# Two FFNs with seven products over all row blocks, and the residual kept in DRAM

## Chip, cores and metric

One core of a Trainium2 chip. The metric is device time in microseconds, here a median of 3 runs. TensorE multiplies, ScalarE (ACT), VectorE (DVE) and GpSimd (POOL) work on elements, SyncE (SP) issues most DMAs. Each engine works through its own queue in order.

## The reference

Two transformer blocks over 1024 tokens of width 1024, in float32. What this change touches are the output projection of the first block's attention, and the two feed-forward networks (FFNs):

```
x = x + g1 * (concat(norm(o_a), norm(o_b)) @ w_out)            # output projection
x = x + g2 * ((silu(h @ w_gate) * (h @ w_up)) @ w_down)        # first FFN; h = modulated norm of x
x = x + gla(norm(x))                                           # second block's mixer
u = causal_conv3(norm(x) @ ffn_w_up) + b; g, val = split(u)    # second FFN
x = x + (silu(g) * val) @ ffn_w_down                           # then the final norm
```

Both FFNs have 2816 hidden columns: 11 groups of 256. Each full-precision product is three matmuls (high part by high, high by low, low by high), with every operand cut into a rounded high part and a rest.

## The kernel before, in words

**Residual and activations.** `X` holds the residual x as eight tiles of 128 rows in SBUF. `H[0]` and `H[1]` hold the high and low parts of the normed activations, transposed, as 8 blocks of 128 rows (k) by 1024 tokens.

**Weights (class `Weights`, L62).** `W` is a planner with a list of tasks in a fixed order: for each item a load of 1 MB into `raw` (one buffer, L159), then its pieces, then an end. A piece takes the next of the 8 slots of a ring (`ring`), if its owner has released it, and is cut there into high (ACT, L139) and low parts (DVE or POOL, L140). `W.tick(n)` emits up to n tasks at the place where it is called; a load is emitted with the tick that ends the item before it, and with `W.pause` the tick after a load does nothing. `need(idx, j)` and `get` emit at once what is still missing. Since `raw` is one buffer, a load waits on SP until the last piece of the item before has been cut. The order in an FFN is gate of g, down of g-1, up of g.

**FFN (`ffn`, L1451).** `first` computes group 0 of gate and up in plain products: tokens 0 to 511 first, then 512 to 1023. Groups 1 to 9 run as `seven(g, "g")`, `down(g - 1)`, `seven(g, "u")`. `seven` replaces the eight block products of [2 column halves x 2 row halves of the weights] by [2 row halves x 2 token halves of H] with seven products of sums (Winograd's form of Strassen's method). Before, that is done on k blocks 0 to 3 only (each product over 2 blocks); blocks 4 to 7 go as plain products: 14 + 16 = 30 block products of three matmuls, 90 in all. The weight sums are made by POOL (`_seven`, L100: 256 columns per operation), in 6 pieces. The sums over H are made once per FFN by `t_step0` to `t_step4` during `first`'s second half and the first `seven`, and overwrite part of H's second half; `restore` brings that back at group 9. The results are put together by DVE sums from PSUM (L1674), POOL sums (L1677) and ACT copies (L1670) in six buffers `uv`.

**Places in `seven`.** After each product stands `point(i)`: `STEPS` (L33) says how many waiting output stages it emits (`flush`: convolution taps, SiLU, multiplication, cutting of the hidden values) and how many weight tasks (`W.tick`):

```
(False, 'g'): ((2, 0), (0, 1), (0, 2), (0, 2), (1, 2), (1, 0), (1, 0)),
(False, 'u'): ((1, 1), (0, 1), (1, 0), (0, 1), (2, 2), (0, 2), (3, 1)),
(True, 'g'): ((4, 0), (3, 0), (0, 2), (2, 1), (3, 0), (0, 1), (0, 1)),
(True, 'u'): ((2, 2), (2, 1), (2, 1), (1, 1), (2, 3), (1, 1), (2, 0)),
```

False is the first FFN, True the second (with convolution).

**Down (L1668 on).** 16 outputs of 128x512, each 6 matmuls, added to `X` by `tm_add` (L1377): in the first FFN DVE multiplies by the gate and POOL adds; in the second DVE adds. `down_last` does groups 9 and 10 together and feeds the next norm.

**Output projection (L1427).** Four column quarters `n4`, each over 8 row tiles; the norm of the result (`Norm`, 14 steps) runs along the last quarter and into `first`.

Of the kernel before, what the change touches and what calls it, by code (L numbers as in the profile page):

```python
# [63 lines left out]
class Weights:  # L64
# [24 lines left out]
    def add7(self, load):  # L89


        idx = len(self.items)
        self.items.append({"load": load, "done": False, "slots": []})
        self.tasks.append(("load", idx, 0))
        for j in range(6):
# [117 lines left out]
def kernel(ctx: ExitStack, tc: tile.TileContext, a: dict, out: bass.AP, dbg=None):  # L213
# [1005 lines left out]
    xp = pool("x", "right", stack=st_x)  # L1219
    X = [xp.tile([P, D], F32, tag=f"x{t}", name=f"x{t}") for t in range(8)]  # L1220
    hp = pool("hT", "right", stack=st_x)
    H = [hp.tile([P, KD, S], R32, tag=f"h{i}", name=f"h_{i}") for i in range(2)]
    st_ps = ExitStack()
# [17 lines left out]
    class Norm:  # L1241
# [177 lines left out]
    nrm = Norm(dmod[2], lambda t, xh: to_fm(None, xh, t), dmod[1])  # L1419
# [7 lines left out]
    for n4 in range(4):  # L1427
# [8 lines left out]
        for t in range(8):  # L1436
# [21 lines left out]
    def ffn(tag, conv, grow, nrm, nxt):  # L1458
# [8 lines left out]
        W.tmp = fp.tile([P, 2, 2, P], F32, name="s12")  # L1467
# [107 lines left out]

# [3 lines left out]
        def hb(x, k, half):  # L1579
            return H[x][:, 2 * k:2 * k + 2, half * 512:half * 512 + 512]  # L1580

        def hf(x, k, half):
            return hb(x, k, half).bitcast(F32)

        def open_t():
            tp = pool("t" + tag, "right", stack=st_t)
            T["t"] = [tp.tile([P, 2, 2, 512], R32, name=f"t{x}") for x in range(2)]
            tp = pool("t2" + tag, "right", stack=st_t2)
            T["t2"] = [tp.tile([P, 2, 512], R32, name=f"t2{x}") for x in range(2)]
# [8 lines left out]
        def t_step0():  # L1598
            tt(nc.gpsimd, f3, hf(1, 0, 1), hf(1, 0, 0))
            tt(nc.vector, f1, hf(0, 0, 1), hf(0, 0, 0))  # L1600
            tt(nc.vector, f1, f1, f3, ALU.add)

        def t_step1():
            tt(nc.vector, f2, hf(0, 1, 1), f1)
            tt(nc.vector, f2, f2, hf(1, 1, 1), ALU.add)
            t_split(f2, *T["t2"])

        def t_step2():
            W.tick(2)
            tt(nc.vector, f3, f2, hf(0, 0, 0))  # L1610
            tt(nc.gpsimd, f3, f3, hf(1, 0, 0))
            tt(nc.vector, f2, hf(0, 1, 0), f2)
            tt(nc.gpsimd, f2, f2, hf(1, 1, 0), ALU.add)

        def t_step3():
            t_split(f1, *[hb(x, 0, 1) for x in range(2)])

        def t_step4():
            t_split(f3, *[t[:, 0] for t in T["t"]])
            t_split(f2, *[t[:, 1] for t in T["t"]])  # L1620
# [580 lines left out]
```

## Time and profile before

| what | value |
|---|---|
| median of 3 runs | 2676.56 us (2676.5 to 2678.79) |
| profiled execution, its own time | 2675.95 us |
| its span, first to last instruction | 2674.2 us |
| granted TensorE clock, mean | 0.991 |
| output projection | to 734 us |
| first FFN | 734 to 1467 us |
| second FFN | 1906 us to the end |

The span is what the trace covers; 1.75 us of the execution lie outside. In rows, L12 is line 12 of the kernel; `out<-in` are tile names; a number in square brackets is the idle time of the engine before that instruction, with what ended it. A group is one pass of the loop over g: one `seven` for up, one for the next gate, one `down`, as they follow each other from one end of a `down` to the next.

### The profile page before, as it was taken

The numbers are of one execution on the slowest core, as the hardware profiler recorded it, in microseconds if no ns is written. First come the engines' busy times: TensorE is split into PE (matmuls) and PEld (weight loads), VectorE is DVE, ScalarE is ACT, GpSimd is POOL, SyncE is SP. The second block draws the span as 40 slices with busy tenths as digits, with TensorE's granted clock in tenths as the row PEclk, the third lists the DMA queues.
The fourth block names the chain that finished last, engine by engine and source line by source line (L and its number), as shares of the span: only waits on it lengthen the run. The fifth ranks groups of instructions, "written<-read, shape, count | busy, mean of one in ns | idle before, by whom it ended". The sixth has DMA issues, their size and how long they took to land. (4 is left out here: it accounts for less than half of the span.)

```text
span 2674.2 us, 37149 instructions
## 1 busy us (share of the span) xinstructions
PE 2575.6 (96%) x14053; PEld 2152.5 (80%) x14053; DVE 1631.4 (61%) x3011; ACT 1057.8 (40%) x2613; POOL 1139.3 (43%) x1079
## 2 busy tenths in 40 slices
PE   8999999999899999999999999999999999999998
PEld 4999898899887888888878877877777777777786
DVE  4688678774475555555556442332777777777766
ACT  4644488784232222222223525232433333333333
POOL 2355255664446666666643111212333333333321
PEclk9999999999999999999999999999999999999999
DMA  6166422212101111111111111111101111111112
GB/s 244 33 194 203 144 52 68 64 44 88 56 17 48 63 48 48 54 57 48 48 48 56 35 48 32 48 32 48 40 32 48 48 48 48 48 48 48 48 48 87
DMA packets 152540, 170.87 MB, mean 64 GB/s; under 512 B 39444, under 2 KB 135460, under 8 KB 151336
## 3 DMA queue, kind: packets, MB, share of 16 engines
q1 hardware_dynamic: 152200, 168.35, 19.9%
q8 instruction: 111, 1.82, 0.3%
q0 software_dynamic: 160, 0.14, 0.1%
q14 instruction: 69, 0.57, 0.1%
HBM read 154.81 MB, written 13.65 MB: 63 GB/s over the span
## 5 line engine op out<-in xcount | busy, mean ns | idle before, releaser
L140 POOL TENSOR_TENSOR wlo<-raw,whi 128x512 fp32r<-128x512 f32 x132 | 178.8, 1359 | 449.1 <-ACT whi L139 420.2
L1656 PE MATMUL pgu<-h,whi 128*128 128x512 f32 x864 | 342.6, 397 | 3.1 <-DVE h L1592 3.1
L1657 PE MATMUL pgu<-h,wlo 128*128 128x512 f32 x864 | 341.2, 395 | 0.5 <-POOL wlo L140 0.5
L1655 PE MATMUL pgu<-h,whi 128*128 128x512 f32 x864 | 341.3, 395 | 0.0
L140 DVE TENSOR_TENSOR wlo<-raw,whi 128x512 fp32r<-128x512 f32 (+2 forms) x304 | 230.1, 769 | 153.4 <-ACT whi L139 152.8
L139 ACT ACTIVATE whi<-raw 128x512 fp32r<-128x512 f32 (+1 forms) x436 | 232.5, 552 | 170.9 <-DMA raw<-in_w_down 60.3
L1674 DVE TENSOR_TENSOR uv<-pgu,uv 128x512 f32<-128x512 f32 x216 | 148.3, 687 | 150.2 <-PE pgu L1657 129.2
L237 PE MATMUL pdn<-wlo,hid 128*128 128x512 f32 x576 | 227.3, 395 | 12.2 <-DVE wlo L140 12.2
L236 PE MATMUL pdn<-whi,hid 128*128 128x512 f32 x576 | 226.3, 393 | 1.2 <-DVE uv L1383 1.1
L238 PE MATMUL pdn<-whi,hid 128*128 128x512 f32 x576 | 226.5, 393 | 0.0
L1384 POOL TENSOR_TENSOR x<-x,uv 128x512 f32<-128x512 f32 x144 | 192.2, 1356 | 32.2 <-DVE uv L1383 29.3
L1656 PEld LDWEIGHTS pgu<-h,whi 128*128 128x128 f32 x864 | 162.2, 188 | 42.3 <-DVE h L1592 3.6
L1655 PEld LDWEIGHTS pgu<-h,whi 128*128 128x128 f32 x864 | 162.5, 188 | 40.1
L1657 PEld LDWEIGHTS pgu<-h,wlo 128*128 128x128 f32 x864 | 162.2, 188 | 39.9 <-POOL wlo L140 0.9
L1525 POOL TENSOR_TENSOR hid<-sg,hid 128x512 fp32r<-128x512 f32 x80 | 106.8, 1340 | 194.3 <-ACT hid L1524 192.2
L1677 POOL TENSOR_TENSOR uv<-uv 128x512 f32<-128x512 f32 x72 | 106.4, 1478 | 162.9 <-DVE uv L1674 162.9
L236 PE MATMUL pin<-whi,h 128*128 128x256 f32 x512 | 145.5, 284 | 5.4 <-ACT hsq L634 2.2
L237 PE MATMUL pin<-wlo,h 128*128 128x256 f32 x512 | 145.6, 284 | 1.7 <-DVE wlo L140 1.7
L238 PE MATMUL pin<-whi,h 128*128 128x256 f32 x512 | 145.7, 285 | 0.0
L1524 ACT ACTIVATE hid<-sg 128x512 fp32r<-128x512 f32 x80 | 50.3, 632 | 231.9 <-DVE sg L1522 231.9
L237 PEld LDWEIGHTS pdn<-wlo,hid 128*128 128x128 f32 x576 | 108.1, 188 | 41.7 <-DVE wlo L140 17.3
L236 PEld LDWEIGHTS pdn<-whi,hid 128*128 128x128 f32 x576 | 108.1, 188 | 27.1 <-DVE uv L1383 1.5
(391 smaller groups left out, 6985.2 us busy)
## 6 DMA issues: line engine op xcount, KB each, us to landing
raw<-in_ffn_w_up SPq DMA_DIRECT2D x22, 1024.0 KB
mraw<-in_w_mod SPq DMA_DIRECT2D x32, 512.0 KB
raw<-in_w_gate SPq DMA_DIRECT2D x11, 1024.0 KB
raw<-in_w_up SPq DMA_DIRECT2D x11, 1024.0 KB
raw<-in_w_down SPq DMA_DIRECT2D x11, 1024.0 KB
raw<-in_ffn_w_down SPq DMA_DIRECT2D x11, 1024.0 KB
raw<-in_w_in SPq DMA_DIRECT2D x9, 1024.0 KB
wm<-in_w_mod SPq DMA_DIRECT2D x8, 1024.0 KB
```

The costliest lines, as they stand in the source:

```text
L139: nc.scalar.activation(out=hi, in_=src, func=AF.Copy)
L140: (engine or self.engine or nc.vector).tensor_tensor(out=lo, in0=src, in1=hi.bitcast(F32), op=ALU.subtract)
L236: nc.tensor.matmul(ps, lh, rh, start=(i == 0), stop=False)
L237: nc.tensor.matmul(ps, lh, rl, start=False, stop=False)
L238: nc.tensor.matmul(ps, ll, rh, start=False, stop=(i == n - 1))
L1384: nc.gpsimd.tensor_tensor(out=xs, in0=xs, in1=tmp, op=ALU.add)
L1525: nc.gpsimd.tensor_tensor(out=hl[:, c], in0=sg[:, cc, c], in1=hh[:, c].bitcast(F32), op=ALU.subtract)
L1655: nc.tensor.matmul(ps, lh, rh, start=start and k == 0, stop=False)
L1656: nc.tensor.matmul(ps, lh, rl, start=False, stop=False)
L1657: nc.tensor.matmul(ps, ll, rh, start=False, stop=stop and k == n - 1)
L1674: nc.vector.tensor_tensor(out=o, in0=ps, in1=u, op=ALU.add)
L1677: nc.gpsimd.tensor_tensor(out=o, in0=u, in1=v, op=ALU.add)
```

## The change

- `seven` takes seven products over all 8 row blocks: 7 x 4 = 28 block products, 84 matmuls. Each weight item has seven pieces of 4 blocks (one slot each); POOL's sums run over 512 columns; the low parts of pieces 1, 5 and 6 are made by POOL, of the others by DVE. The sums over H are made for all 8 blocks, in two halves r = 0, 1. `STEPS` stays as it is.
- In an FFN, x stands in DRAM (`xd`). Before `first` eight DMAs on SP write it, `X` is closed and its space used for the sums over H; after group 9 eight DMAs read it back. In `down` the output goes to one of six buffers (first FFN: DVE, times the gate; second: ACT copy), and a DMA issued by POOL adds it to `xd` in DRAM, issued one output later.
- Quarters 2 and 3 of the output projection run in pairs of row tiles; the norm that follows (`LongNorm`) has 12 steps, giving row tile t four steps after the step that squares it where before it was six.
- In the second FFN the first tap of each output is put one place earlier into the list of waiting stages.

```diff
@@ -100,21 +100,20 @@
     def _seven(self, it, j):
         nc = self.nc
         r = it["raw"][:, :2048].rearrange("p (k c) -> p k c", k=8)
-        a11, a21, a12, a22 = r[:, 0:2, 0:P], r[:, 0:2, P:2 * P], r[:, 2:4, 0:P], r[:, 2:4, P:2 * P]
+        a11, a21, a12, a22 = r[:, 0:4, 0:P], r[:, 0:4, P:2 * P], r[:, 4:8, 0:P], r[:, 4:8, P:2 * P]
         s1, s2 = self.tmp[:, 0], self.tmp[:, 1]
         tt = nc.gpsimd.tensor_tensor
         n = it["slots"][-1]
         if j == 0:
             tt(out=s1, in0=a21, in1=a22, op=ALU.add)
             tt(out=a21, in0=a11, in1=a21, op=ALU.subtract)
+        elif j == 1:
             tt(out=s2, in0=s1, in1=a11, op=ALU.subtract)
-        parts = [(a11, s1), (a12, s2), (r[:, 4:8, 0:P],), (s2, a21), (a22,), (r[:, 4:8, P:2 * P],)][j]
-        for i, src in enumerate(parts):
-            w = 4 if j in (2, 5) else 2
-            hi, lo = [x[:, n, 256 * i:256 * i + w * P].rearrange("p (k c) -> p k c", k=w) for x in self.ring]
-            self.split(hi, lo, src, None, nc.gpsimd if w == 4 else nc.vector)
-        if j == 1:
+        elif j == 4:
             tt(out=s2, in0=a12, in1=s2, op=ALU.subtract)
+        src = (a11, a12, s1, s2, s2, a21, a22)[j]
+        hi, lo = [x[:, n, 0:4 * P].rearrange("p (k c) -> p k c", k=4) for x in self.ring]
+        self.split(hi, lo, src, None, nc.gpsimd if j in (1, 5, 6) else nc.vector)
...
+    X = [None] * 8
+    xs = {"n": 0}
+    def open_x():
+        xs["st"] = ExitStack()
+        xp = pool(f"x{xs['n']}", "right", stack=xs["st"])
+        xs["n"] += 1
+        X[:] = [xp.tile([P, D], F32, tag=f"x{t}", name=f"x{t}") for t in range(8)]
+    open_x()
     st_ps = ExitStack()
     ps_a = pool("ps_a2", space=PSUM, stack=st_ps)
...
+    class LongNorm(Norm):
+        def __init__(self, *args):
+            super().__init__(*args)
+            self.steps = 12
+        def give_next(self):
+            t = self.pos - 4
+            if 0 <= t < 8:
+                self.give(t, self.xh.pop(t))
+        def work(self):
+            k = self.pos
+            self.pos += 1
+            if 0 <= k - 2 < 8 and k % 2 == 0:
+                self.root(k - 2, 2)
+            if 0 <= k - 2 < 8:
+                self.scale(k - 2)
+            if 1 <= k < 9:
+                xr = self.xh[k - 1] = self.pl.tile([P, D], F32, tag="xh", name="xh", bufs=3)
+                nc.gpsimd.tensor_tensor(out=xr, in0=X[k - 1], in1=self.rows[0], op=ALU.mult)
+            if k < 8:
+                self.square(k)
+            if k == 11:
+                self.stack.close()
...
                 wo_mm(ps[:, :256], t, wi, wl, 4, 8)
             W.tick()
             tm_add(mp, t, n4 * 256, 256, ps[:, :256], gb)
+    ws = [[kc8(w) for w in W.get(ids["wo", 2])]]
+    for t0 in range(0, 8, 2):
+        pss = [ps_a.tile([P, 512], F32, tag="acc", name="pwo", bufs=4) for _ in range(2)]
+        for n in range(2):
+            if len(ws) <= n:
+                ws.append([kc8(w) for w in W.get(ids["wo", 3], True)])
+            if n == 1 and t0 == 6:
+                W.release(ids["wo", 2])
+            for i in range(2):
+                wo_mm(pss[i][:, n * 256:n * 256 + 256], t0 + i, *ws[n], 0, 8)
+                if n == 0 and t0 == 0 or n == 1 and t0 == 6:
+                    W.tick(2)
+                if n == 1:
+                    nrm.give_next()
+                    tm_add(mp, t0 + i, 512, 512, pss[i], gb)
+                    nrm.work()
...
+            xs["st"].close()
             tp = pool("t" + tag, "right", stack=st_t)
+            T["t"] = [tp.tile([P, 2, 4, 512], R32, name=f"t{x}") for x in range(2)]
             tp = pool("t2" + tag, "right", stack=st_t2)
+            T["t2"] = [tp.tile([P, 4, 512], R32, name=f"t2{x}") for x in range(2)]
+            T["f"] = (f2, tp.tile([P, 2, 512], F32, name="f3"))
+            T["x"] = tp.tile([P, 512], F32, name="xpart")
...
+        def parts(i, r):
+            return [(x[:, i - 1] if i else y)[:, 2 * r:2 * r + 2] for x, y in zip(T["t"], T["t2"])]
+        def t_step0(r):
+            f1, f3 = uv[:, 2 * r:2 * r + 2], T["f"][1]
+            tt(nc.gpsimd, f3, hf(1, 0, 1, r), hf(1, 0, 0, r))
+            tt(nc.vector, f1, hf(0, 0, 1, r), hf(0, 0, 0, r))
             tt(nc.vector, f1, f1, f3, ALU.add)
+        def t_step1(r):
+            tt(nc.vector, f2, hf(0, 1, 1, r), uv[:, 2 * r:2 * r + 2])
+            tt(nc.vector, f2, f2, hf(1, 1, 1, r), ALU.add)
+        def t_step2(r):
+            f2, f3 = T["f"]
+            tt(nc.vector, f3, f2, hf(0, 0, 0, r))
+            tt(nc.gpsimd, f3, f3, hf(1, 0, 0, r))
+            tt(nc.vector, f2, hf(0, 1, 0, r), f2)
+            tt(nc.gpsimd, f2, f2, hf(1, 1, 0, r), ALU.add)
+        def t_part(i, r):
+            t_split(T["f"][i % 2], *parts(i, r))
+        def t_first(r):
+            t_split(uv[:, 2 * r:2 * r + 2], *[hb(x, 0, 1, r) for x in range(2)])
+        def t_run(*steps):
+            def f():
+                for g_, *args in steps:
+                    g_(*args)
+            return f
...
+        t_steps = [t_run((t_step0, 0), (t_step1, 0), (t_part, 0, 0)),
+                   t_run((t_step2, 0), (t_part, 1, 0), (t_part, 2, 0), (t_step0, 1)),
+                   t_run((t_step1, 1), (t_part, 0, 1), (t_step2, 1)),
+                   t_run((t_first, 0), (t_first, 1))]
+        t_last = [t_run((t_part, 1, 1)), t_run((t_part, 2, 1))]
...
+                if conv and later:
+                    later.insert(len(later) - 1, f.pop(0))
...
+                if g == 1 and kind == "g" and i < 2:
+                    t_last[i]()
                 if g == NG - 2 and kind == "u":
                     restore(i)
                 W.tick(nt)
+            p1 = copy(prod(0, hr(0, 0), True))
             point(0)
+            ps = prod(1, hr(4, 0))
+            p5 = copy(prod(2, hr(0, 1), True))
             point(1)
+            p6 = prod(3, tr_(0), True)
             u2 = new()
             add(u2, p6, p1)
             add(p1, ps, p1)
...
             u4 = new()
             add_sb(u4, u2, p5)
             point(2)
+            ps = prod(4, hr(4, 1))
             add(u4, ps, u4)
             late(0, 1, u4)
             point(3)
+            p7 = prod(5, tr_(1), True)
             add(u2, p7, u2)
             add_sb(p5, u2, p5)
             point(4)
+            ps = prod(6, tr_(2))
             add(u2, ps, u2)
             late(1, 0, u2)
             point(5)
             late(1, 1, p5)
             point(6)
+        pend = []
+        def x_part(t, cc, ps):
+            a0 = turn[0] - 4
+            f3 = T["f"][1]
+            tmp = (f3[:, 0], f3[:, 1], T["x"], uv[:, a0 % 6], uv[:, (a0 + 4) % 6], uv[:, (a0 + 5) % 6])[(2 * t + cc) % 6]
+            c = slice(cc * 512, cc * 512 + 512)
+            if gbt is None:
+                nc.scalar.activation(out=tmp, in_=ps, func=AF.Copy)
+            else:
+                nc.vector.tensor_tensor(out=tmp, in0=ps, in1=gbt[:, c], op=ALU.mult)
+            x_send()
+            pend.append(lambda: nc.gpsimd.dma_start(out=xd[t][:, c], in_=tmp, accum_op=ALU.add))
+        def x_send():
+            while pend:
+                pend.pop(0)()
...
                     mm3(ps, [(hd[k][0][:, t * P:(t + 1) * P], hd[k][1][:, t * P:(t + 1) * P],
                               wi[:, k, cc * 512:(cc + 1) * 512], wl[:, k, cc * 512:(cc + 1) * 512])
                              for k in range(2)])
+                    x_part(t, cc, ps)
                 flush(STEPS[conv, "d"][t][0])
                 W.tick(STEPS[conv, "d"][t][1])
+            x_send()
...
+        up = pool("uv" + tag, "left", stack=st_u)
+        uv = up.tile([P, 6, 512], F32, name="uv")
+        f2 = uv[:, 4:6]
+        W.tmp = up.tile([P, 2, 4, P], F32, name="s12")
...
+        for t in range(8):
+            nc.sync.dma_start(out=xd[t], in_=X[t])
         first()
...
+        open_x()
+        for t in range(8):
+            nc.sync.dma_start(out=X[t], in_=xd[t])
```

## Rows read from the trace of the kernel before

**Rows 1.** Page, part 1: each engine's busy time, share of the span, instructions.
```profile
PE 2575.6 (96%) x14053; PEld 2152.5 (80%) x14053; DVE 1631.4 (61%) x3011; ACT 1057.8 (40%) x2613; POOL 1139.3 (43%) x1079
```

**Rows 2.** Windows view: a first-FFN group, a second-FFN group, `first`'s second half; busy us by engine, clock.
```profile
1029.42:1093.54 64.12, 64.12 (x278) 51.80 (x277) 35.74 (x51) 16.44 (x34) 43.72 (x37) 1.00 0.16 50
2080.57:2148.01 67.44, 64.64 (x278) 51.66 (x276) 48.95 (x79) 22.11 (x42) 24.02 (x20) 1.00 0.14 47
768.75:791.69 22.94, 22.71 (x96) 18.13 (x97) 14.46 (x16) 7.15 (x14) 11.35 (x8) 1.00 0.00 1
```

**Rows 3.** Timeline, TensorE: start, duration, [idle before <- releaser]; first row first FFN, others second.
```profile
1071.39 0.39 PE L236 MATMUL pdn<-whi,hid 128*128 128x512 f32 x1
...
2115.78 0.51 PE L1655 MATMUL pgu<-t,whi 128*128 128x512 f32 x1 [1.46 <-DVE uv L1674]
...
2126.70 0.50 PE L237 MATMUL pdn<-wlo,hid 128*128 128x512 f32 x1 [1.34 <-DVE wlo L140]
```

**Rows 4.** Waits view, TensorE, whole span: us in total, times, longest.
```profile
PE pdn L237 <- DVE wlo L140: 12.2, 11, 1.4
...
PE tp L241 <- DVE h L1239: 5.7, 2, 4.1
...
PE pgu L1656 <- DVE h L1592: 3.1, 1, 3.1
```

**Rows 5.** Timeline, SP queue: start of each load of the raw weights.
```profile
1039.18 0.37 SPq L294 DMA_DIRECT2D raw<-in_w_gate  x1
1060.11 0.37 SPq L302 DMA_DIRECT2D raw<-in_w_down  x1
...
2109.39 0.37 SPq L302 DMA_DIRECT2D raw<-in_ffn_w_down  x1
2127.87 24.91 SPq L294 DMA_DIRECT2D raw<-in_ffn_w_up  x2
```

**Rows 6.** Timeline, POOL: the first operation on the weights loaded from 2127.87 on.
```profile
2133.11 0.75 POOL L108 TENSOR_TENSOR s<-raw 128x256 f32<-128x256 f32 x1 [9.39 <-DMA raw<-in_ffn_w_up]
```

**Rows 7.** Lines view, whole span: busy us, mean ns of one | idle before, releasers.
```profile
L139 ACT ACTIVATE whi<-raw 128x512 fp32r<-128x512 f32 (+1 forms) x436 | 232.5, 552 | 170.9 <-DMA raw<-in_w_down 60.3 <-DMA raw<-in_ffn_w_up 51.6 <-DMA raw<-in_w_up 21.0
...
L140 POOL TENSOR_TENSOR wlo<-raw,whi 128x512 fp32r<-128x512 f32 x132 | 178.8, 1359 | 449.1 <-ACT whi L139 420.2 <-PE pgo L237 23.6 <-ACT eg L1973 5.3
L1525 POOL TENSOR_TENSOR hid<-sg,hid 128x512 fp32r<-128x512 f32 x80 | 106.8, 1340 | 194.3 <-ACT hid L1524 192.2 <-PE pgu L238 2.1
L1677 POOL TENSOR_TENSOR uv<-uv 128x512 f32<-128x512 f32 x72 | 106.4, 1478 | 162.9 <-DVE uv L1674 162.9
...
L1674 DVE TENSOR_TENSOR uv<-pgu,uv 128x512 f32<-128x512 f32 x216 | 148.3, 687 | 150.2 <-PE pgu L1657 129.2 <-POOL uv L1677 19.7
```

**Rows 8.** Timeline, VectorE, second FFN: a late sum, and one operation short and long.
```profile
2115.04 1.41 DVE L1674 TENSOR_TENSOR uv<-pgu,uv 128x512 f32<-128x512 f32 x2
...
2119.49 0.74 DVE L1503 SCALAR_TENSOR_TENSOR cv<-uv,vec,cv 128x511 f32<-128x511 f32 x1
...
2122.48 1.79 DVE L1503 SCALAR_TENSOR_TENSOR cv<-uv,vec,cv 128x511 f32<-128x511 f32 x1 [0.19 <-ACT cv L1499]
```

**Rows 9.** Line L1592 (the sums over H), ns min/median/max; and its last write into H.
```profile
L1592 DVE TENSOR_TENSOR t<-uv,t x6: 1211/1225/2359, 782.3 to 1978.7; 128x1024 fp32r<-128x1024 f32 x6
...
L1592 POOL TENSOR_TENSOR uv<-uv,h x4: 3364/3390/3432, 792.0 to 1970.5; 128x1024 f32<-128x1024 f32 x4
...
793.07 3.42 DVE L1592 TENSOR_TENSOR h<-uv,h 128x1024 fp32r<-128x1024 f32 x1
```

**Rows 10.** Queues (packets, MB, share of 16 engines); POOL-issued loads (KB, us to landing), one's issue.
```profile
q1 hardware_dynamic: 152200, 168.35, 19.9%
...
qg<-in_kn_b POOLq DMA_DIRECT2D x1, 32.0 KB, 7.6
sink<-in_sink_a POOLq DMA_DIRECT2D x1, 4.0 KB, 3.7
...
L430 POOL DMA_DIRECT2D sink<-in_sink_a x1 | 0.8, 760 | 0.0
```

More of the change, by code (lines that the diff above doesn't have):

```diff
@@ L94, in add7 @@
         self.tasks.append(("load", idx, 0))
-        for j in range(6):
+        for j in range(7):
             self.tasks.append(("seven", idx, j))
@@ L1218 @@
     st_x = ExitStack()
-    xp = pool("x", "right", stack=st_x)
-    X = [xp.tile([P, D], F32, tag=f"x{t}", name=f"x{t}") for t in range(8)]
     hp = pool("hT", "right", stack=st_x)
     H = [hp.tile([P, KD, S], R32, tag=f"h{i}", name=f"h_{i}") for i in range(2)]
+    xd = dram.tile([NT, P, D], F32, name="xd")
+    X = [None] * 8
[6 more added lines that the diff above has]
+    open_x()
     st_ps = ExitStack()
@@ L1426 @@
     early = {}
-    for n4 in range(4):
+    for n4 in range(2):
         wi, wl = W.get(ids["wo", n4])
@@ L1596, in t_split @@
             tt(nc.vector, lo, f, hi.bitcast(F32))
-        def t_step0():
-            tt(nc.gpsimd, f3, hf(1, 0, 1), hf(1, 0, 0))
-            tt(nc.vector, f1, hf(0, 0, 1), hf(0, 0, 0))
-            tt(nc.vector, f1, f1, f3, ALU.add)
[L1603 to L1620, printed above, removed]
+        def parts(i, r):
[4 more added lines that the diff above has]
+            tt(nc.vector, f1, hf(0, 0, 1, r), hf(0, 0, 0, r))
+            tt(nc.vector, f1, f1, f3, ALU.add)
+        def t_step1(r):
[16 more added lines that the diff above has]
+            return f
         def restore(i):
+            b = [x[:, 0:4, 0:512].bitcast(F32) for x in H]
+            o = [x[:, 0:4, 512:1024] for x in H]
             if i == 3:
@@ L1626, in restore @@
                 bp = pool("b12" + tag, "right", stack=st_t2)
-                T["b"] = [bp.tile([P, 2, 512], F32, name=f"b12{x}") for x in range(2)]
-                tt(nc.gpsimd, T["b"][1], hf(1, 0, 1), hf(1, 0, 0), ALU.add)
-                tt(nc.vector, T["b"][0], hf(0, 0, 1), hf(0, 0, 0), ALU.add)
+                T["b"] = [bp.tile([P, 4, 512], F32, name=f"b12{x}") for x in range(2)]
+                tt(nc.gpsimd, T["b"][1], o[1].bitcast(F32), b[1], ALU.add)
+                tt(nc.vector, T["b"][0], o[0].bitcast(F32), b[0], ALU.add)
             elif i == 5:
                 tt(nc.vector, T["b"][0], *T["b"], ALU.add)
-                t_split(T["b"][0], *[hb(x, 0, 1) for x in range(2)])
-        t_steps = [t_step0, t_step1, t_step2, t_step3]
+                t_split(T["b"][0], *o)
+        t_steps = [t_run((t_step0, 0), (t_step1, 0), (t_part, 0, 0)),
[3 more added lines that the diff above has]
+        t_last = [t_run((t_part, 1, 1)), t_run((t_part, 2, 1))]
         def flush(n):
@@ L1643, in seven, with prod, hr @@
             idx = ids[tag, kind, g]
[L1645 to L1647 removed]
+            def prod(j, rhs, on_t=False):
+                if on_t:
+                    ps = ps_t.tile([P, 512], F32, tag="tp", name="pgu", bufs=2)
+                else:
                     ps = ps_a.tile([P, 512], F32, tag="acc", name="pgu", bufs=4)
[L1649 to L1651 removed]
                 sl = W.need(idx, j)
                 for k, (rh, rl) in enumerate(rhs):
[L1654 to L1655 removed]
+                    lh, ll = [x[:, k * P:(k + 1) * P] for x in sl]
+                    nc.tensor.matmul(ps, lh, rh, start=(k == 0), stop=False)
                     nc.tensor.matmul(ps, lh, rl, start=False, stop=False)
[L1657 removed]
+                    nc.tensor.matmul(ps, ll, rh, start=False, stop=(k == 3))
+                W.release(idx, j)
                 return ps
[L1660 removed]
+            def hr(k0, half):
                 c = slice(half * 512, half * 512 + 512)
[L1662 removed]
+                return [(H[0][:, k, c], H[1][:, k, c]) for k in range(k0, k0 + 4)]
             def tr_(i):
                 t = [x[:, i - 1] for x in T["t"]] if i else T["t2"]
[L1666 removed]
+                return [[x[:, k] for x in t] for k in range(4)]
             def copy(ps):
@@ L1789, in new @@
             return uv[:, (turn[0] - 1) % 6]
+        for t in range(8):
+            nc.sync.dma_start(out=xd[t], in_=X[t])
         first()
-        gt = SimpleNamespace(tile=new)
         W.pause = True
```

51 lines of the change are left out of this document (7 added, 44 removed).

## The prediction, made blind

> **What bounds the kernel now.** The page's engine table comes first: TensorE is busy for 2575.6 of 2674.2 us [rows 1], so it leaves less than 100 us idle in all. The windows view then separates the stages. A group of the first FFN lasts 64.12 us, one of the second 67.44 us, at a granted clock of 1.00; VectorE is busy for 48.95 us of the second [rows 2]. The timeline gives the pitch: from 1029.42 to 1071.39 us run two `seven` calls of 90 matmuls, so one takes 41.97/180 = 0.2332 us; the `down` lasts to 1093.54, 22.15 us [rows 2, 3]. Without a stall a group would last 64.1 us in either FFN. The first is there; the second loses 3.3 us per group, mostly to the two waits of 1.46 and 1.34 us shown [rows 3].
>
> So the FFNs run at TensorE's pace, as long as weights are cut in time. The queue view tells by how much. In the first FFN `up` starts at 1029.42 and the next gate's load is issued at 1039.18, 9.76 us into it; `down`'s load at 1060.11, 9.7 us into the gate that starts at 1050.41 [rows 2, 5]. A load takes 5.24 us from issue (2127.87) to the first operation on its data (2133.11) [rows 5, 6]. Landing 15.0 us into a call of 21.0, it has 6 us of slack. Each load waits for the last piece of the item before, because there is one `raw` buffer. That slack is what the change spends.
>
> **The change, part by part.**
>
> *Matmuls.* 90 become 84 per call: 36 calls x 6 x 0.2332 = 50.4 us less TensorE work, all on the path, 2.8 us per group. A product now is 12 matmuls, 2.80 us; a call 19.6 us.
>
> *Weights of the first FFN.* The ring has 8 slots and `down` holds 4, so only four pieces of `up` can be cut during `down`. Of the rest there were two, now three. `STEPS` puts one tick at points 0, 1 and 3: the seventh piece is emitted at point 3. Its low part is POOL's, behind two others in POOL's queue. Product 3 ends 11.2 us into the call; three DVE operations (0.69 each) and an ACT operation (0.55) must follow before the hidden value's low part at 13.8, and that takes 1.34; then the piece, 1.36: `raw` is free at 16.5 [rows 7]. The load lands at 21.7, ACT cuts the first high part by 22.3, and the call ended at 19.6: TensorE waits 2.7 us, and some 0.4 more for the low part. The landing would have to be 2.7 us earlier.
>
> Next, the second product of the gate needs the sums s1, a21, s2 and a low part on POOL, four operations of 1.36 us (at 512 columns [rows 7]), done 5.4 us after landing, 27.1; its third matmul is due at 22.7 + 2.8 + 0.5 = 26.0: 1.1 to 1.4 us. Pieces 5 and 6 of the gate come at point 2, behind DVE's sum (0.69) and POOL's (1.48): `raw` is free 0.69 + 1.48 + 2 x 1.36 = 4.9 us after product 3, `down`'s load lands at 10.1, the first high part is there at 10.7, and the call ends at 8.4: 2.3 us. `down`'s first two outputs need all four pieces, cut one after the other, with DVE's sums of products 5 and 6 between them in its queue (they are emitted after the first piece, which waits for the load): 4 x 0.69 + 2 x 0.69 = 4.1 us, of which 1.4 go beside matmuls at least and at most all but 1.7. Together 2.3 + (1.7 to 3.7) = 4 to 6; I take 5.5. Sum per group: 3.1 + 1.4 + 0.3 + 5.5 = 10.3 of stalls less 2.8: +7.5, nine groups +68 (bounds +45 and +72).
>
> *Weights of the second FFN.* Here `up` has ticks 2, 1 at points 0 and 1, so the gate's load is early. The sum s2 and the low part of piece 1, though, stand on POOL behind p7's sum and a hidden low part: 0.5 to 3 us of wait for product 1, I take 2.5. Pieces 5 and 6 come at point 2 again, on engines that run late: the sums of the product that ended near 2109.96 (36 matmuls after 2101.56) start at 2115.04, 5.1 us behind [rows 8]. DVE gives up 16 additions (16 x 0.69 = 11 us per `down`) to ACT, so I take 2.2 us late instead of 5.1: product 5 waits 3.6 (0.3 to 5.3), `down` 2.5 for its load and 1.0 for its low parts. In `down`, ACT copies now stand behind the first cut of `up`, which waits for a load issued some 2.6 us into `down`: 5.24 us of block against four PSUM buffers of 1.38 us each: 0 to 3, I take 2.5. Stalls 12.1, less 2.8, less the 3.3 of before, which these take the place of: +6.0 per group, nine groups +54 (bounds -21 and +78).
>
> *POOL and DVE contention.* The same DVE operation takes 0.74 us and 1.79 us within 3 us [rows 8]; POOL's sum has a mean of 1.48 against 1.36 for like shapes [rows 7]. The Trainium skill ("SBUF — State Buffer", "Who interferes with whom") says that a DVE instruction with two SBUF inputs and a POOL instruction that reads SBUF exclude each other. By it each of four POOL operations in the second FFN's chain would take 0.45 us more, +1.8 per group, and the sum would be 16 us higher. The trace agrees in direction; that all four meet a neighbour no row shows.
>
> *Sums over H.* They double: ten more DVE operations of 1.22 us per FFN, two more POOL ones of 3.39 [rows 9]. Before, the last write into H ends at 793.07 + 3.42 = 796.5, and the product that reads it was due 5.6 us after 791.69, at 797.3; in the second FFN it was 3.1 us late already [rows 4, 9]. DVE has 8.5 us idle in that window [rows 2]. So the delay lies between 12.2 - 8.5 = 3.7 and 12.2 + 6.8 = 19 us; I take 10, twice: +20.
>
> *x in DRAM.* The write, 4.19 MB, goes at 168.35 MB/(0.199 x 2674.2 us) = 316 GB/s [rows 10]: 13 us within the first half of `first`, which lasts from 734 to 768.75. Read back, it stands ahead of the last `up` load: 13.3 + 5.24 + 0.55 = 19.1 against 22.4 us of matmuls: hidden, 3 us spare. Group 10's gate comes late in the first FFN as the others do: +3. Each accumulation leaves POOL after 0.76 us of issue [rows 10]; POOL gets 14 operations of 512 columns and 12 us of issues per group where the adds took 21.7: not full. Six buffers carry the transfers if one output's share, 1.38 us, suffices. The plain rate gives 0.83 us for 256 KB, twice that (read, add, write) 1.66; landing was 3.7 to 7.6 us for what POOL issued before [rows 10]. (7.6 + 0.76 + 0.69 + 1.38)/6 = 1.74. So between 0 and (1.74 - 1.38) x 16 x 18 = +103 us; I take 0, by the plain rate. The Trainium skill ("DMA: Bandwidth & Descriptors", "Anatomy of one DMA — SWDGE (gpsimd) path") fits 2.0 us + bytes/436e3, as an estimate 2.6 us per accumulation; by it the buffers come round in 0.9 us and the sum stays. No run here shows it.
>
> *Output projection and tap.* The matmuls stay. The wait of 5.7 us for blocks of the norm [rows 4] should go, as blocks are given earlier; what may come is a wait for the third quarter's partner, whose last four pieces are emitted at once: -5 (-8 to +3). The moved tap: 0.
>
> **Sum**: 68 + 54 + 20 + 3 - 5 = +140. 2675.95 + 140 = 2816; the median stands 0.6 above the profiled execution: 2817 us.
>
> **The rivals.**
>
> *Weights keep up: faster.* If the load were issued 2.7 us earlier in each call of the first FFN, and no queue made up new waits, TensorE's saving would stand: -50, -5, +4 for the H sums: 2625 us. For it speaks that nothing but order is short: POOL and ACT have idle time in every group [rows 2]. Against it, `STEPS` is the same and each load hangs on the last of seven pieces. It decides at 13.8 us into the call.
>
> *The accumulations bind.* At 1.74 us per output, as above: +103, 2920 us. The small packets of the rows shown were loads at another place in the kernel, so they bound it only.
>
> *Each accumulation waits for the one before it*, for all write `xd`: then 16 x (3.7 + 0.76) = 71 us per `down` in place of 22, +800 us or more. That the slices don't overlap speaks against it.
>
> **How the numbers follow.** Chances: forecast 0.66, with its own range of 2740 to 2860 (the bounds of all its terms together would give 2700 to 2870, and hardly stand at one end all at once); accumulations bind 0.14; faster 0.12; serial accumulations 0.05; no change 0.03. The range of 2725 to 2985 leaves out the faster rival and the serial one. A change of 0.2% (5 us) is about what can be told. Faster 0.12, same 0.03, slower 0.85.
>
> **What would show it.** Right: in the first FFN the gate's load is issued near 16.5 us into `up` (9.76 before); TensorE waits for `whi` of the gate and for `whi`, `wlo` of `down`; groups of about 71.5 and 73.5 us; pitch still 0.233. The first `seven` waits some 10 us for `h` of the H sums. Wrong: no wait of TensorE on weights, groups near 61.3 us. If TensorE waits for PSUM in `down`, with DVE or ACT waiting for DMAs into `xd`, the second rival holds.

## The result, and the profile after

The changed kernel takes 2916.2 us (median; 2913.2 to 2920.5) beside 2677.7 us of the kernel before on the same chip: 1.089 times as long, interval 1.087 to 1.091. The forecast was 2817: slower, as measured, but 99 us short. The profiled execution spans 2917.0 us, 242.8 more than before. The parts of it follow, from the starts of TensorE's instructions in the timelines (us). f1 and f2 are the first and the second FFN, "first gate product" is the first call of `seven` (the gate of group 1), e7 and e11 are experiments below:

| stretch | before | after | e7 | e11 |
|---|---|---|---|---|
| f1: first gate product | 21.0 | 52.8 | 58.3 | 35.1 |
| f1: first `down` to the last `up` | 537.3 | 627.0 | 526.7 | 526.4 |
| f1: last `up` and group 10 | 67.3 | 83.5 | 68.0 | 68.0 |
| f2: first gate product | 27.4 | 59.6 | 55.2 | 42.3 |
| f2: first `down` to the last `up` | 564.3 | 626.9 | 555.9 | 532.6 |
| f2: last `up` and group 10 | 65.7 | 73.6 | 79.4 | 72.2 |
| all else in the span | 1391.2 | 1393.6 | 1396.2 | 1394.4 |

The page's first part, of the changed kernel (busy us, share, instructions), answers to [rows 1]:

```profile
PE 2644.3 (91%) x13837; PEld 2162.8 (74%) x13837; DVE 1606.6 (55%) x2735; ACT 1165.2 (40%) x2693; POOL 1373.9 (47%) x1257
```

TensorE has 216 matmuls less (36 calls of 6, as forecast) and yet 69 us more busy time. So it has not only waited; its matmuls took longer. The windows view shows both, for a group of f1, a group of f2 and the two first gates (columns as in [rows 2]):

```profile
1021.26:1096.32 75.06, 68.40 (x265) 52.43 (x264) 36.15 (x42) 17.14 (x30) 45.14 (x40) 0.91 0.49 99
2411.34:2486.36 75.02, 66.62 (x265) 51.33 (x264) 40.42 (x54) 32.13 (x54) 46.02 (x38) 0.95 0.48 99
792.07:844.88 52.81, 28.51 (x86) 20.47 (x84) 30.02 (x22) 12.20 (x18) 25.75 (x14) 0.71 0.06 20
2102.09:2161.65 59.56, 30.75 (x84) 21.92 (x85) 37.64 (x35) 16.05 (x24) 26.28 (x14) 0.66 0.05 18
```

No engine is full: POOL is busy for 45 of 75 us, DVE for 36 to 40. But the granted clock, 1.00 in every group before, is 0.91 and 0.95. In the first gates it is 0.71 and 0.66, where it was 1.00 and 0.94. The timeline of TensorE says when it falls (an f1 group of the changed kernel):

```profile
1040.84 0.40 PE L1723 MATMUL pgu<-t,wlo 128*128 128x512 f32 x1
1044.53 0.79 PE L1721 MATMUL pgu<-h,whi 128*128 128x512 f32 x1 [3.29 <-ACT whi L138]
1045.12 0.63 PE L1722 MATMUL pgu<-h,whi 128*128 128x512 f32 x1
...
1049.71 0.63 PE L1723 MATMUL pgu<-h,wlo 128*128 128x512 f32 x1
1050.13 0.47 PE L1721 MATMUL pgu<-h,whi 128*128 128x512 f32 x1
1050.44 0.39 PE L1722 MATMUL pgu<-h,whi 128*128 128x512 f32 x1
```

Behind a wait of 3.29 us twelve matmuls start 0.43 to 0.6 us apart instead of 0.23. In the windows view that stretch stands at a granted clock of 0.50, the lower level (1.2 GHz), with TensorE busy throughout:

```profile
1044.60:1049.40 4.80, 4.80 (x11) 3.35 (x12) 4.80 (x5) 1.38 (x3) 4.72 (x4) 0.50 0.00 0
1050.00:1061.00 11.00, 11.00 (x48) 8.83 (x48) 4.52 (x5) 3.80 (x7) 5.77 (x6) 0.99 0.01 1
```

So a stall can be paid twice. I added up, over the six stretches above, the idle times in TensorE's timeline (stalls), and what the distance between starts has over 0.2335 us (slow products). Stalls: 30 us before, 199 after. Slow products: 9 before, 130 after. +169, +120 and the -50 of matmuls saved make 239 of the 240 us by which the six stretches grew. Some 95 of the 120 us lie where the trace's clock records stand at 0.50; the rest stands at 1.00.

What TensorE waited for (waits view of the changed kernel, whole span; us in total, times, longest):

```profile
PE pgu L1721 <- ACT whi L138: 80.8, 24, 15.0
PE pgu L1723 <- POOL wlo L139: 47.3, 25, 6.9
PE pdn L235 <- ACT whi L138: 23.4, 16, 3.4
PE pdn L236 <- DVE wlo L139: 20.9, 32, 1.7
PE pgu L1723 <- DVE wlo L139: 14.4, 7, 6.7
```

All five lines are waits for pieces of weights, 187 us together. SP's queue shows the loads of the group that starts with `up` at 1021.26:

```profile
1038.61 0.37 SPq L293 DMA_DIRECT2D raw<-in_w_gate  x1
1063.45 0.37 SPq L301 DMA_DIRECT2D raw<-in_w_down  x1
```

The gate's load is issued 17.4 us into `up` (9.8 before, by [rows 5]; 16.5 forecast). The accumulating DMAs stand in three views of the changed kernel: the queues (SP's and POOL's: packets, MB, share of 16 engines), the DMA issues (KB, us from issue to landing), and ACT's waits:

```profile
q1 hardware_dynamic: 156808, 185.13, 19.7%
q0 software_dynamic: 41632, 75.65, 16.3%
```

```profile
xd<-uv POOLq DMA_DIRECT2D x126, 256.0 KB, 6.7
xd<-f POOLq DMA_DIRECT2D x108, 256.0 KB, 6.7
```

```profile
ACT uv L1799 <- DMA xd<-uv: 52.8, 32, 4.5
```

75.65 MB in 16.3% of 16 engines' span are 9.9 GB/s an engine, against 20.1 for q1: 1.65 us for 256 KB, twice the plain price (the upper bound of the prediction had 1.66). The waits for a buffer to come free stand mostly on ACT and are short (4.5 us at most in this row); TensorE waits 3.2 us in all for ACT's copies in `down`.

### The profile page after: what moved, and what is told of

Its sections match the earlier page's. It is cut to its first block, busy times and chain, and to the rows that moved or that the text cites. A ratio compares the mean times of both kernels' runs of the same rounds, so it can differ in the third digit from the quotient of the medians.

```text
span 2917.0 us, 37189 instructions
## 1 busy us (share of the span) xinstructions
PE 2644.3 (91%) x13837; PEld 2162.8 (74%) x13837; DVE 1606.6 (55%) x2735; ACT 1165.2 (40%) x2693; POOL 1373.9 (47%) x1257
## 3 DMA queue, kind: packets, MB, share of 16 engines
q0 software_dynamic: 41632, 75.65, 16.3%
## 5 line engine op out<-in xcount | busy, mean ns | idle before, releaser
L139 POOL TENSOR_TENSOR wlo<-raw,whi 128x512 fp32r<-128x512 f32 x168 | 244.1, 1461 | 390.8 <-ACT whi L138 361.9
L1721 PE MATMUL pgu<-h,whi 128*128 128x512 f32 x576 | 244.6, 425 | 67.5 <-ACT whi L138 67.5
L139 DVE TENSOR_TENSOR wlo<-raw,whi 128x512 fp32r<-128x512 f32 (+1 forms) x196 | 171.1, 901 | 240.8 <-ACT whi L138 240.8
L1723 PE MATMUL pgu<-h,wlo 128*128 128x512 f32 x576 | 244.4, 424 | 35.5 <-POOL wlo L139 22.3
L1722 PE MATMUL pgu<-h,whi 128*128 128x512 f32 x576 | 242.5, 421 | 0.0
L139 DVE TENSOR_TENSOR wlo<-s,whi 128x512 fp32r<-128x512 f32 x108 | 108.8, 1013 | 181.5 <-ACT whi L138 181.5
L1723 PE MATMUL pgu<-t,wlo 128*128 128x512 f32 x432 | 179.9, 416 | 26.2 <-POOL wlo L139 25.0
L1721 PEld LDWEIGHTS pgu<-h,whi 128*128 128x128 f32 x576 | 118.0, 205 | 101.0 <-ACT whi L138 73.9
L1744 POOL TENSOR_TENSOR uv<-uv 128x512 f32<-128x512 f32 x72 | 105.1, 1459 | 186.2 <-DVE uv L1741 186.2
L1721 PE MATMUL pgu<-t,whi 128*128 128x512 f32 x432 | 177.5, 411 | 14.7 <-ACT whi L138 13.4
L1722 PE MATMUL pgu<-t,whi 128*128 128x512 f32 x432 | 176.0, 407 | 0.0
L1803 POOL DMA_DIRECT2D xd<-f x108 | 115.5, 1336 | 115.0 <-ACT f L1799 71.5
L235 PE MATMUL pin<-whi,h 128*128 128x256 f32 x512 | 146.0, 285 | 5.7 <-ACT hsq L633 2.0
```

The costliest lines, as they stand in the source:

```text
L139: (engine or self.engine or nc.vector).tensor_tensor(out=lo, in0=src, in1=hi.bitcast(F32), op=ALU.subtract)
L235: nc.tensor.matmul(ps, lh, rh, start=(i == 0), stop=False)
L1721: nc.tensor.matmul(ps, lh, rh, start=(k == 0), stop=False)
L1722: nc.tensor.matmul(ps, lh, rl, start=False, stop=False)
L1723: nc.tensor.matmul(ps, ll, rh, start=False, stop=(k == 3))
L1744: nc.gpsimd.tensor_tensor(out=o, in0=u, in1=v, op=ALU.add)
```

## The experiments

Two theories stood first: W, the weights (pieces cut late hold `raw`, so loads come late), and A, the accumulations.

**e1, the accumulations left out.** The 288 accumulating DMAs are not issued; the middle blocks' products never reach x.

```diff
-            pend.append(lambda: nc.gpsimd.dma_start(out=xd[t][:, c], in_=tmp, accum_op=ALU.add))
+            pass
```

> The changed kernel with the 144 accumulating DMAs of each FFN not issued (the products of the middle row blocks then never reach x; the copies of them stay). Theory W (the weights bind: one raw tile, seven pieces of which the last are cut late, so that the next load starts too late for its first product): the waits of PE for whi and wlo stay, a group of gate, down and up goes from 75.1 to 69-75 us, since only the POOL time of the issues (16 x 1.34 us a group) comes free for pieces cut on POOL; the time is 2810 to 2910 us. Theory A (the accumulations bind, by their transfer of 16 x 1.65 us a group or by holding the loads up): the waits for whi and wlo go, groups fall to about 62-64 us, the time to about 2690-2720 us. The waits in the first gate product stay by both.

2904.8 us, 11 less than the changed kernel. Groups: 75.1 us in f1, 73 to 75 in f2. The waits for weights stay (waits view of e1), so A is out:

```profile
PE pgu L1721 <- ACT whi L138: 80.1, 23, 15.1
PE pgu L1723 <- POOL wlo L139: 47.3, 25, 6.9
```

**e2, the loads left out.** Pieces are cut from old content.

```diff
-            it["raw"] = self.pool.tile([P, MAXE], F32, tag="raw", name="raw", bufs=1)
-            it["load"](it["raw"])
+            if self.pause: it["raw"] = self.items[t[1] - 1]["raw"]
+            else: ...
```

> The changed kernel with the weight loads of the middle row blocks (down 0 to up 9 of each FFN) not issued: the pieces are cut again and again from the raw tile's old content, so that cutting, slots and products stay and only the loads and the wait for them go. Theory W: the waits for whi and wlo at the start of each product go, f1 groups fall from 75.1 to 62-67 us, f2 groups from 75.0 to 65-73 us, and the granted clock in the groups rises to 0.97 or more; the time is 2720 to 2830 us. Theory A (accumulations): groups stay above 73 us, the time above 2890 us. The first gate products (52.8 and 59.6 us) stay.

2855.2 us: above the range of W and under that of A. f1 groups are 68.4 us, f2 groups 74.3: without any load most of the loss stays. W in its first form, a load that lands too late, explains some 6.7 us per group of f1 and hardly anything of f2. The rest was to be sought in the cutting.

**e3, the first gate reordered.** Four pieces ahead of the sums, the splits into `h` ahead of step2 of the second half.

```diff
-                            W.tick(2)
+                            W.tick(4)
-        t_last = [t_run((t_part, 1, 1)), t_run((t_part, 2, 1))]
+        t_last = [t_run((t_step2, 1), (t_part, 1, 1)), t_run((t_part, 2, 1))]
```

> The changed kernel with four pieces of the first gate block cut (instead of two) ahead of the H sums of the second half, the splits into h put ahead of the last sums, and step2 of the second half of the sums moved behind the first product of the seven. Theory Q (the first gate waits because its third and later pieces, and the h that its third product reads, stand in the ACT and DVE queues behind the H sums): the 11.74 us and 5.42 us waits shrink, the first gate products take 25 to 35 us instead of 52.8 and 59.6, the time is 2850 to 2880 us. Rival S (the H sums themselves are the work that ends late, whatever their order): less than 10 us is won in each FFN, the time is 2898 to 2917 us. The groups after it stay at 75 us by both.

2896.3 us. First gates 41.3 and 49.8 us: 11.5 and 9.8 won, between the two expectations. TensorE now waits for `h` in one piece (waits view of e3, first gate of f1), so the sums were late themselves:

```profile
PE pgu L1721 <- ACT h L1647: 8.9, 1, 8.9
```

Why, the changed kernel's own queues show (timelines of POOL, DVE and ACT around the 11.74 us wait that ends at 816.60):

```profile
809.42 3.31 POOL L1644 TENSOR_TENSOR uv<-uv,h 128x1024 f32<-128x1024 f32 x1
...
807.18 6.64 DVE L1644 TENSOR_TENSOR h<-uv,h 128x1024 fp32r<-128x1024 f32 x2
813.74 0.68 DVE L1571 TENSOR_TENSOR sg<-pgu,sg 128x512 f32<-128x512 f32 x1
...
814.45 0.63 ACT L1573 ACTIVATE hid<-sg 128x512 fp32r<-128x512 f32 x1 [3.22 <-DVE sg L1571]
814.99 1.04 ACT L1647 ACTIVATE t<-f 128x1024 fp32r<-128x1024 f32 x1
815.93 0.61 ACT L138 ACTIVATE whi<-s 128x512 fp32r<-128x512 f32 x1
```

Read upwards from the piece: it stands behind a split and a hidden value on ACT, these behind a product on DVE, that behind two writes into `h`, which take 3.3 us each while POOL is at work on its part of the sums.

**e6, the sums on DVE alone**, in that order:

```diff
-            tt(nc.gpsimd, f3, hf(1, 0, 1, r), hf(1, 0, 0, r))
-            tt(nc.vector, f1, f1, f3, ALU.add)
+            tt(nc.vector, f1, f1, hf(1, 0, 1, r), ALU.add)
+            tt(nc.vector, f1, f1, hf(1, 0, 0, r))
```

(likewise in step2.)

> The order of e3_first_gate, and the H sums made by DVE alone (three subtractions or additions in a row of 1.22 us each in place of two on DVE and one of 2.3 to 3.4 us on POOL). Theory H (in the first gate the time goes in hand-overs between DVE and POOL, and in DVE operations that take 2.2 us instead of 1.22 while POOL reads SBUF): the first gate products fall to 23-32 us (52.8 and 59.6 in the changed kernel, 41.3 and 49.8 in e3_first_gate), the time is 2845 to 2870 us. Rival S (the sums bind by their amount: 26 DVE operations of 1.22 us a half, behind units of the first block that need DVE too): the first gates stay at 36-45 us, the time at 2875 to 2895 us. Groups stay at 75 us by both.

2883.7 us, first gates 34.3 and 43.5: near the boundary, and by its time (2875 to 2895) rival S. Taking POOL out wins 7.0 and 6.3 us although DVE gets more operations; then DVE's amount binds. The lines view of the same line, changed kernel first (ns min/median/max):

```profile
L1644 DVE TENSOR_TENSOR h<-uv,h x4: 3355/3359/3362, 807.2 to 2124.6; 128x1024 fp32r<-128x1024 f32 x4
```

```profile
L1644 DVE TENSOR_TENSOR h<-uv,h x4: 1216/1218/1218, 800.3 to 2094.5; 128x1024 fp32r<-128x1024 f32 x4
```

The Trainium skill ("SBUF — State Buffer", "Who interferes with whom") has it that a DVE instruction with two SBUF inputs and a POOL instruction that reads SBUF exclude each other. These rows agree: 3.36 us beside POOL's operations, 1.22 in e6, where POOL's timeline has no operation during them.

**e5, the low halves on DVE.**

```diff
-        self.split(hi, lo, src, None, nc.gpsimd if j in (1, 5, 6) else nc.vector)
+        self.split(hi, lo, src)
```

> The changed kernel with the lo halves of pieces 1, 5 and 6 made by DVE (0.69 us each) instead of POOL (1.3 us each, in POOL's queue between accumulation issues of 1.34 us). Theory P (besides the load, the waits for wlo are POOL's queue: the lo halves of pieces 1, 5 and 6 stand behind other POOL work, and the last of them also holds raw and so the next load): the waits for POOL wlo (47 us in all) go, f1 groups fall from 75.1 to 68-72 us, f2 groups from 75.0 to 71-74 us, the last up of f1 from 30.2 to 22-25 us; the time is 2820 to 2870 us. Rival D (DVE is as late as POOL): groups within 1 us of 75, the time 2900 to 2920 us. The first gate products change by under 8 us by both.

2878.2 us, between the two ranges. Groups 72.8 and 71.7. TensorE's waits for POOL's pieces go, but those for DVE's on the same line grow from 14.4 us to 43.8:

```profile
PE pgu L1723 <- DVE wlo L139: 43.8, 29, 6.8
```

f1 keeps a wait of 2.9 us for `whi` in a group, and its last `up` takes 29.2 us, not 22 to 25. POOL's queue is a part, not the cause.

**e8, both on DVE**, and three of the four parts of the sums handed out ahead of the first block's units:

```diff
+                        if half == 1 and len(t_steps) > 1:
+                            t_steps.pop(0)()
                         unit(...)
+                    W.tick(1)
                     t_last[i]()
```

> e5_lo_dve and e6_hsums_dve together; further, three of the four parts of the H sums are handed out before the unit of the first block rather than behind its silu or product, which wait for PE in DVE's queue, and one piece is cut ahead of each of the two last parts. STEPS as in the changed kernel. If the two causes (lo halves on POOL; H sums late) are apart, their gains add: 38 and 33 us, and the earlier hand-out takes the first gate products from 34.3 and 43.5 us to 24-32: the time is 2825 to 2850 us. If both were the same DVE or POOL time, DVE, which takes over both, is late and the time is 2860 us or more.

2838.6 us: the gains of e5 and e6 add (38 + 33, and 7 on top). The first gates, 33.2 and 41.3 us, hardly gain on e6; the 24 to 32 expected of the earlier hand-out were missed.

**e7, another order alone.** The changed kernel with other entries in `STEPS` (stages handed out, pieces cut, at each point):

```diff
-    (False, 'g'): ((2, 0), (0, 1), (0, 2), (0, 2), (1, 2), (1, 0), (1, 0)),
-    (False, 'u'): ((1, 1), (0, 1), (1, 0), (0, 1), (2, 2), (0, 2), (3, 1)),
-    (False, 'd'): ((1, 0), (0, 0), (0, 1), (0, 0), (0, 2), (0, 2), (0, 3), (0, 1)),
+    (False, 'g'): ((0, 0), (3, 0), (0, 0), (0, 0), (1, 1), (0, 0), (0, 0)),
+    (False, 'u'): ((0, 2), (0, 2), (1, 2), (0, 0), (0, 2), (0, 3), (0, 1)),
+    (False, 'd'): ((0, 0), (0, 0), (0, 1), (0, 0), (0, 1), (0, 0), (1, 0), (2, 2)),
+    (True, ...): ...
```

> The changed kernel with another STEPS table alone: the same pieces, loads and stages, but cut and handed out at other points of the three products of a group, so that the pieces of an item are cut earlier and its raw tile comes free before the next item's first product needs the load. Theory O (the order in the queues, not the amount of work of any engine, makes PE wait): of the 13.7 us that an f1 group takes over its PE work (6.6 us of stalls, 7.1 us of products at the lower clock behind them) at least half goes, groups fall to 62-68 us in f1 and 65-71 us in f2, the time is 2730 to 2830 us. Rival W1 (one raw tile: a load of 6 to 10 us from free to landed between any two items binds, whatever the order): groups stay at 72 us or more, the time at 2890 us or more. The first gate products stay within 6 us of 52.8 and 59.6.

2741.1 us, 175 less than the changed kernel. f1 groups are 62.7 us, f2 groups 66.2. The windows of one of each:

```profile
1063.15:1125.89 62.74, 61.61 (x266) 49.50 (x265) 33.32 (x42) 17.27 (x30) 45.50 (x40) 1.00 0.58 118
2407.18:2473.32 66.14, 62.41 (x265) 49.16 (x264) 41.50 (x54) 31.77 (x54) 45.83 (x39) 1.00 0.52 111
```

Set these beside the rows of the changed kernel: the same counts of instructions on every engine (but for one at a window's edge), POOL 45.5 us instead of 45.1, and 12.3 us less in f1, at a clock of 1.00. The gate's load goes out 11.1 us into `up`:

```profile
1074.27 0.37 SPq L293 DMA_DIRECT2D raw<-in_w_gate  x1
```

One `raw` tile is enough; W1 is out, and theory O stands: what was short was neither an engine nor a queue of DMAs, but the place of the pieces in the queues.

**e9, all of it together**, with a table for the version on DVE.

> e8_dve_both with a STEPS table drawn up for it. By theory O the groups come near their PE work of 61.6 us: 62-66 us in f1, 63-68 us in f2, against 64.1 and 67.4 of the kernel before; the time is 2665 to 2725 us, so that this version may end on either side of the kernel before (2678). By rival W1 (the load into one raw tile binds) groups stay at 70 us or more and the time above 2800 us.

2773.2 us: outside both. f2 groups run in 62.9 us, f1 groups in 73.4 (windows view):

```profile
1294.45:1367.62 73.17, 67.07 (x265) 52.06 (x264) 36.11 (x48) 16.80 (x30) 37.04 (x34) 0.93 0.49 102
2454.39:2517.29 62.90, 61.87 (x266) 49.43 (x264) 44.49 (x61) 31.68 (x54) 36.11 (x34) 1.00 0.56 118
```

The FFN with less work on DVE (36 us a group) is the one that stalls. Whether f1's table is at fault or its low halves on DVE, as in e5 (72.8 us), this run doesn't tell.

**e10, the better order for each FFN**: f1 as in e7, f2 as in e9, first gates as in e8.

```diff
-        self.split(hi, lo, src)
+        self.split(hi, lo, src, None, nc.gpsimd if j in self.on_pool else nc.vector)
+        W.on_pool = () if conv else (1, 5, 6)
```

> e8_dve_both with its first gate kept, and for each FFN the order that ran better: f1 with the lo halves of pieces 1, 5 and 6 on POOL and the f1 table of e7_steps, f2 with all lo halves on DVE and the f2 table of e9_all. Theory O (each FFN's groups depend on its own order alone): f1 groups 62.7 us as in e7_steps, f2 groups 62.9 us as in e9_all, first gates 33-37 and 41 us as in e8_dve_both: 2741 - 9 x 3.2 (f2 groups) - 6 (f2 plain) - 23 - 14 (first gates) = 2669 us, range 2660 to 2685, level with the kernel before (2678) or under it. If the gains of the two tables hang on each other or on the first gate's tail, the time is 2690 us or more.

2676.8 us, 0.9996 of the kernel before (0.9987 to 1.0005); groups 62.7 and 62.9, first gates 38.7 and 41.2. Each FFN's groups go by their own order.

**e11, the late sums behind the first and third product.**

```diff
-        t_last = [t_run((t_step2, 1), (t_part, 1, 1)), t_run((t_part, 2, 1))]
+        t_last = [t_run((t_step2, r), (t_part, 1, r), (t_part, 2, r)) for r in range(2)]
```

(The hand-out of the earlier sums and their buffers change with it.)

> e10_mix with the sums that only the sixth and seventh product read (step2 of both halves and their splits, 14.6 us of DVE in all) handed out behind the first and the third product of the first gate, not ahead of the splits into h that the third product reads. By theory S (DVE's queue ahead of the third product is 5 to 7 us too long) the waits of 5.7 and 7.1 us for h and of 4.9 us for the first piece go, and the first gates take 24-30 us in place of 33 and 41: the time is 2645 to 2662 us, under e10_mix by 8 to 22 us and under the kernel before. If the sixth product then waits for its sums as long as the third did, the time is within 5 us of e10_mix.

2673.0 us: 0.9983 of the kernel before (0.9974 to 0.9992), so 0.2% under it, the best version here, and 3.8 us under e10. That is the second outcome expected, not the 2645 to 2662 us of theory S. The first gates take 35.1 and 42.3 us, not 24 to 30: the waits for `h` are shorter, the sixth and seventh product wait instead.

**e12, all seven pieces early.**

```diff
-                    W.tick(1)
+                    W.tick(3 - 3 * i)
```

> e11_mix_late with pieces 5, 6 and 7 of the first gate block all cut behind its first product, ahead of the late sums, so that the raw tile comes free there and the weights of the first down are loaded some 10 to 20 us earlier. In e11_mix_late the first gates and the downs behind them took 59.6 us in f1 and 72.1 us in f2, with 10.4 and 18.7 us of stalls, half of them on whi or wlo. Theory O (order of the queues) expects most of these waits on whi and wlo to go: 3 to 6 us less in f1 and 6 to 14 us less in f2, the time 2655 to 2666 us. Rival S (the DVE time of the late sums, 14.6 us, binds the sixth product whatever stands ahead of it): the waits turn from whi and wlo into waits for t, and the time stays within 3 us of 2673 us.

2733.5 us, 60 more and outside both. f1 does as theory O says (first gate 28.6 us, its groups unchanged). In f2 the first gate with its `down` is 9 us shorter too, and then every group takes 71.6 us instead of 62.9. A group's window and two loads of SP's queue, of e11 and then of e12:

```profile
2225.86:2288.69 62.83, 61.89 (x265) 49.41 (x264) 42.57 (x61) 31.67 (x54) 35.40 (x32) 1.00 0.55 114
```

```profile
2255.73 0.37 SPq L301 DMA_DIRECT2D raw<-in_ffn_w_down  x1
2267.49 0.37 SPq L293 DMA_DIRECT2D raw<-in_ffn_w_up  x1
```

```profile
2237.16:2308.80 71.64, 65.25 (x265) 51.41 (x264) 42.20 (x60) 32.12 (x54) 36.33 (x33) 0.95 0.52 100
```

```profile
2269.26 0.37 SPq L301 DMA_DIRECT2D raw<-in_ffn_w_down  x1
2286.01 0.37 SPq L293 DMA_DIRECT2D raw<-in_ffn_w_up  x1
```

The loads are issued 29.9 and 41.6 us after the group's first product in e11, 32.1 and 48.9 in e12: the same table, at another position in the list of pieces. f2's table hands out 21 ticks per group for 18 pieces and three pauses behind loads, none to spare, so a shift stays; f1's hands out 17 and leaves the rest to the product that needs them, which brings it back in step. That this is why only f2 kept the shift fits, but wasn't tried. Nor was e11 with early pieces in f1 alone.

**e4, the output projection alone**, in the kernel before:

```diff
-    nrm = Norm(dmod[2], ...)
+    nrm = LongNorm(dmod[2], ...)
```

(with the paired products of the last two quarters.)

> The kernel before with the paired output projection and its longer norm alone, nothing of the FFNs. Theory: the stage from the first output-projection product to the first gate product is 3 to 4 us shorter, the time is 4 us under the kernel before (0.998 to 0.999 of it). Rival: the norm's last steps land on the first gate product instead, and the time is within 1 us of before or above it.

2674.8 us, 0.9992 of before (0.9982 to 1.0002): as expected in size, not told from no change. The path was another, though. From the first product of the output projection to the first matmul of `first` (group 0's gate) it is 99.0 us instead of 105.1, 6.1 less. The first half of `first` then takes 39.4 us instead of 34.8, with a wait that the kernel before lacks (waits view of e4, 640 to 770 us):

```profile
PE pgu L238 <- DVE wlo L140: 4.3, 1, 4.3
```

So most of the gain is given back, much as the rival says, by a piece of weights instead of the norm; the changed kernel has the same two lengths.

## Why the prediction was right in sign and 99 us short

- *Matmuls, -50.4.* Right: 216 fewer, and the pitch of 0.23 us holds where the clock is 1.00; behind long waits it doesn't.
- *Weights of the first FFN, +68.* The mechanism held (load at 17.4 us, waits for `whi` and `wlo`, group longer), the size did not: a group is 75.1 us instead of 71.5. The stalls were even put too high, 10.3 us a group against 6.6: the gate's first product waits 3.3 us (3.1 forecast), its second not at all (1.4), `down` 3.2 (5.5). Two slips are in that sum: 4.1 less the 1.4 beside matmuls leaves 2.7, not 3.7, so 5.5 lies above `down`'s own bound of 5.0, and no row is given for the 0.3. What the sum lacked is 7.1 us of slow products behind the stalls. +90 in all by the table, above the bound of +72.
- *Weights of the second FFN, +54.* 75.0 us a group instead of 73.5, in all +63: stalls 8.3 (12.1 forecast) and 5.2 of slow products. The waits of the gate's products 1 and 5 (counted from 0) came as forecast (2.6 and 3.6 us against 2.5 and 3.6), but `down` waits 1.7 us instead of 3.5, and behind ACT's copies TensorE waits 0.2 us instead of 2.5. f1 can do without nearly all of its loss at the same work (62.7 us in e7), f2 without most of it (66.2 us; 62.9 with the low halves on DVE, e9 and e11), so the rival "weights keep up" had a real condition; with this table it wasn't met.
- *Sums over H, +20.* The worst-sized term: the first gates grew by 32 us each, above the bound of 19. It counted the delay of `h` only. The pieces stand behind the sums in ACT's and DVE's queues (e3), DVE's operations stretch beside POOL's (e6), and the granted clock fell to 0.71 and 0.66. Of each 32, e6 and e8 to e11 had 14 to 20 us back (e12: 24 and 19).
- *x in DRAM, +3.* The accumulations cost 11 us in all (e1), mostly f2's: the transfer took the upper bound, 1.65 us, and 16 of them (26.4 us) are longer than a `down` of 22, but they have the rest of the group to land. An issue took 1.33 us of POOL on average, not 0.76. The rival that they bind is out; groups of 62.7 us carry them as well (e7). Group 10 and the `up` ahead of it grew by 16 and 8 us instead of 3; e7 has f1's share back by order alone, f2's 6.5 us stayed in e11, and no run tells why.
- *Output projection, -5.* Mis-sized: -6.1 us up to the first matmul of `first`, +4.6 in the half that starts there (e4), so -1.5. The moved tap (0) wasn't run alone.

The step that failed is thus one that the prediction did not have: each term priced a wait at its length, and 120 of the 240 us by which the six stretches grew are slow products. With it the stalls as forecast would have overshot. That 2916 us still falls within the stated 2725 to 2985 is luck: it lies outside the forecast's own 2740 to 2860 and above the 2870 that the upper bounds of all its terms give. The range reached so far up for the accumulations, whose 2920 us the result nearly hits and which e1 rules out as the cause.

## What to carry to other kernels

When a tuned order is kept while the pieces behind it change in number, price the order again before the work: 175 of 238 us went by a table alone, with the same instructions on every engine. Price the products behind a stall of TensorE as well as the stall: here 169 us more of stalls came with 120 us more of slow products. And a table of work with no slack seems to keep the offset it starts with (that fits e12, but wasn't tried), so measure a change of the start over the whole loop.

## What was not expected of the hardware

- An accumulating DMA of 256 KB took 1.65 us of the 16 engines (twice the plain rate), 6.7 to 7.1 us from issue to landing, and 0.9 us (median) to 2.7 us of POOL to issue. The Trainium skill ("DMA: Bandwidth & Descriptors", "Anatomy of one DMA — SWDGE (gpsimd) path") would give 2.6 us, as an estimate from its fit; the landing measured here is over twice that, with up to six in flight.
- The clock: behind a wait of 3.29 us, 5.6 us of products at granted clock 0.50; behind one of 2.60 us in a group of f2 (ends at 2436.98) the next products start 0.23 us apart from the second on. Summed over the six stretches, 169 us more of stalls came with 120 us more of slow products.
